# Ten tiles for weight parts, one plain block in the second passes, and side work two steps later in a one-core decoder layer

## The chip, the cores and the metric

The kernel runs on one core of a Trainium2 chip. The metric is the time of one execution on the device in microseconds (us); shown is the median of several executions. The engines are TensorE (PE), VectorE (DVE), ScalarE (ACT), GpSimd (POOL) and SyncE (SP). In this kernel SP issues nearly all transfers (DMAs), in one queue and in order; an issue that waits holds all that are behind it. The other engines, too, work through their instructions in the order of their queue.

## The reference, cut to what matters

One layer of a decoder is computed for 1024 prompt tokens and 64 sample tokens, in single precision:

```python
h = x + 0.5 * rms_norm(swiglu(rms_norm(x, g_f1_pre), w_f1_gu, w_f1_down), g_f1_post)
mix, k_new, v_new, s_new = mixer(rms_norm(h, g_m_pre), ...)
h = h + rms_norm(mix, g_m_post)
h = h + 0.5 * rms_norm(swiglu(rms_norm(h, g_f2_pre), w_f2_gu, w_f2_down), g_f2_post)

def swiglu(x, w_gu, w_down):
    g, u = jnp.split(x @ w_gu, 2, axis=-1)
    return (jax.nn.silu(g) * u) @ w_down
```

The model width is 1024, the hidden width of a SwiGLU 2816, that is 22 blocks of 128. The mixer (stick-breaking attention and retention) lies between the two SwiGLUs; the change touches nothing of it.

## The kernel before, in words

**Three matmuls for one.** Every operand is held as two parts, a high one in a rounded format and the rest. `hi` (L96, on ACT) makes the high part, `lo` (L99, mostly on DVE) the rest, and `mm3` (L133, L137, L138) does a product with three matmuls: high by high, high by low, low by high. To split a weight or an activation is thus one step on ACT and one on DVE.

**Passes and quarters.** A SwiGLU (`ffn`, L693) goes over the tokens in two passes, of 512 and 576 tokens. In a pass the input is cut into four quarters, B11, B21, B12 and B22: the upper or lower half of the model width by the first or second half of the tokens, 256 or 288 columns each. Two weight blocks (f and f + 1) make a round g; a pass has 11 rounds.

**Two kinds of block.** For a block f the product of the gate weights and of the up weights with the input is four quarters of weights by four of input. A *plain* block (`"S1" not in w`, in `swiglu_hidden`) splits four weight quarters, A11, A12, A21 and A22, and does 8 products of quarters. Any other block uses seven products: the weights give A11, A12, A22 and the sums S1 to S4, the input gives B11, B21, B22 and the sums T1 to T4. Each product of quarters is 4 x 3 = 12 matmuls. The weight sums are four operations (L589, L590, L591, L596) on POOL, for blocks 2 and 3 of a first pass on DVE. `PLAIN = 2` (L62) makes blocks 0 and 1 of either pass plain. Split weights go to tiles `sh` and `sl` (L572) in a ring of nine each. A block's generator gives way after its first half and after its second. A plain block has 4 products in either half; another has A11 B11, S2 T2, S3 T3 and S1 T1 in the first, A12 B21, A22 T4 and S4 B22 in the second.

**Where the T come from.** In a first pass DVE makes them from the quarters (`first_sums`, L260). For a second pass they are made on POOL during the first one (`sums`, L244; four operations L251, L253, L255 and L257 for each of four j), stored to the buffer `cB` in DRAM with the quarters, and loaded and split by `late` (L286). `late_sums` (L294) gives these loads in three steps: T2 and T3, T1, T4. T4 uses the buffer of quarter B12 (`HOME`), so it can be loaded only when no product reads B12 any more.

**Second products.** `down` (L706) multiplies a round's two hidden blocks by their rows of the down weights: for each of eight outputs d the products with the first and then with the second block, into banks `pc`; DVE adds the result to `y` (L719), or ACT copies it in the first round. `unit` (L140) loads 512 KB of these weights into a raw tile `wrd` (L146), one of two, and splits it into `whd` and `wld`. A round's `down` stands in the program one round later, between the halves of the next round's first block; only the first round's of a first pass comes before the weights of round 2.

**Side work.** Before the second half of each block a step of a generator is done on the side (`side1`, `side2`), from round 2 on: steps 0 to 19 in a pass. In the second SwiGLU's first pass these are two calls of `boundary` for the tokens of the second pass (norms: squares on ACT, L440, added up on DVE in `acc`, L442; then scaling on DVE, L538, and a sum on POOL or DVE, L540), 8 steps each, and `later_quarters` (L1752), 2 steps, which makes quarters and T for the second pass: 18 steps in all.

**What sets the order.** The program is written out in order, and a scheduler with its own model of durations sets each engine's queue from it; an instruction earlier in the program goes first when several are ready, so blocks and second products are interleaved. `beside` (L116) adds an order by hand: what a step makes on the named engines is put behind the last instruction that each of them had got until then. SP is not among the engines named. Tiles are given out in the scheduler's order, and a tile's next use waits for its last reader.

Of the kernel before, what the change touches and what calls it, by code (L numbers as in the profile page):

```python
# [12 lines left out]
F32R = mybir.dt.float32r  # L13
# [6 lines left out]
P = 128  # L20
# [38 lines left out]
B11, B21, B22, B12, T2, T3, T1, T4 = range(8)  # L59
QUARTERS = (B11, B21, B22, B12)  # L60
HOME = {T4: B12}
PLAIN = 2  # L62

# [3 lines left out]
class Trunk:  # L69
# [70 lines left out]
    def unit(self, src, pool=None, sfx="", eng=None, raw=None):  # L140

        nc = self.nc
        k, c = src.shape[1], src.shape[2]
        raw = self.t(self.wraw, [P, 1024], "wr", bufs=2) if raw is None else self.t(raw, [P, 1024], "wrd", bufs=2)
        rv = raw[:, : k * c].rearrange("p (k c) -> p k c", c=c)
        nc.sync.dma_start(rv, src)  # L146
        pool = pool or self.wsp
        h = self.t(pool, [P, 1024], "wh" + sfx, F32R)
        l = self.t(pool, [P, 1024], "wl" + sfx, F32R)
        self.hi(h[:, : k * c], raw[:, : k * c])  # L150
        self.lo(l[:, : k * c], raw[:, : k * c], h[:, : k * c], eng)
        return (h[:, : k * c].rearrange("p (k c) -> p k c", c=c),
                l[:, : k * c].rearrange("p (k c) -> p k c", c=c))
# [139 lines left out]

    def late_sums(self, u):  # L294
        yield {}
        for bs in ((T2, T3), (T1,), (T4,)):
            for b in bs:
                self.late(u, b)
            yield
# [258 lines left out]
            pass  # L558


    def swiglu_weights(self, wgu, f, adder):


        nc = self.nc
        g = self.t(self.wraw, [P, 1024], "wr", bufs=2)
        v = self.t(self.fw, [P, 1024], "wr2", bufs=2)
        nc.sync.dma_start(g.rearrange("p (k c) -> p k c", c=P), self.cols(wgu, f * P))
        nc.sync.dma_start(v.rearrange("p (k c) -> p k c", c=P), self.cols(wgu, FF + f * P))
        names = ("A11", "S2", "S3", "S1", "A12", "A22", "S4")
        if f < PLAIN:  # L570
            names = ("A11", "A12", "A21", "A22")
        out = {x: [self.t(self.sw, [P, 512], y, F32R, bufs=9) for y in ("sh", "sl")] for x in names}  # L572

        def split(name, src):
            h, l = out[name]
            self.hi(h, src)
            self.lo(l, src, h)
            out[name] = [x.rearrange("p (k c) -> p k c", c=P) for x in (h, l)]

        g0, g1, v0, v1 = g[:, :512], g[:, 512:], v[:, :512], v[:, 512:]  # L580
        tt = adder.tensor_tensor
        split("A11", g0)
        if f < PLAIN:
            split("A12", g1)
            split("A21", v0)
            split("A22", v1)
            return out
        split("A22", v1)
        tt(v1, v0, v1, op=ALU.add)  # L589
        tt(v0, g0, v0, op=ALU.subtract)  # L590
        tt(g0, v1, g0, op=ALU.subtract)  # L591
        split("S2", g0)
        split("S3", v0)
        split("S1", v1)
        split("A12", g1)
        tt(g1, g1, g0, op=ALU.subtract)  # L596
        split("S4", g1)
        return out
# [94 lines left out]
    def ffn(self, q, y, wgu, wdown, chunks, side, begin):  # L693

        nc = self.nc
        with self.fctx as ctx:
            with ExitStack() as ctx2:
                sums = begin(self.pool("fft", ctx2))  # L700
                next(sums)
            dp = self.pool("ffd", ctx, bufs=2)
            self.hp = self.pool("ffh", ctx, bufs=2)
            self.fs = self.pool("ffs", ctx)

            def down(p, g, dw, hid):  # L706
                o0 = PASSES[p][0]
                for o, n in chunks[p] if p or g + 2 < NF else ((0, 256), (256, 256)):
                    c = slice(o - o0, o - o0 + n)
                    for d in range(KD):  # L710
                        dd = slice(d * P, (d + 1) * P)
                        ps = self.bank("pc")
                        for j, ((wh, wl), (hh, hl)) in enumerate(zip(dw, hid)):
                            self.mm3(ps[:, :n], wh[:, 0, dd], wl[:, 0, dd], hh[:, c], hl[:, c],
                                     j == 0, j == len(dw) - 1)
                        if g == 0:
                            nc.scalar.activation(y[p][:, d, c], ps[:, :n], AF.Copy)
                        else:
                            nc.vector.tensor_tensor(y[p][:, d, c], y[p][:, d, c], ps[:, :n], op=ALU.add)  # L719

            for p, (o, n) in enumerate(PASSES):
                before = None
                for g in range(0, NF, 2):
                    if g == 2 and p == 0:
                        before()
                        before = None
                    gens = []
                    begun = {}
                    for f in (g, g + 1):
                        self.beside(lambda: gens.append(self.swiglu_hidden(self.swiglu_weights(  # L730
                            wgu, f, nc.vector if p == 0 and f in (PLAIN, PLAIN + 1) else nc.gpsimd), q, n)),
                            (mybir.EngineType.Activation,) if begun else (mybir.EngineType.DVE,) if self.scaled else (),
                            begun or self.scaled)
                        self.scaled = None
                        if f == 0:
                            next(gens[0])
                            begun = next(sums)
                    next(gens[1 if g == 0 else 0])
                    if before is not None:
                        self.pin = self.last_on(mybir.EngineType.PE)  # L740
                        before()
                        self.pin = None
                    hid = []
                    for i, gen in enumerate(gens):
                        if g == 0:
                            self.beside(lambda: next(sums))
                            if begun and i == 0:
                                begun = self.so_far()
                        else:
                            if i:  # L750
                                next(gen)
                            self.beside(lambda: side(p, g - 2 + i))
                        hid.append(next(gen))
                    if g == 0:
                        self.beside(lambda: next(sums))
                    dw = []
                    for f in (g, g + 1):
                        self.beside(lambda: dw.append(self.unit(
                            wdown[f * P : (f + 1) * P, :].rearrange("p (k c) -> p k c", k=1), pool=dp, sfx="d",
                            raw=self.fw)), PINNED if begun else (), begun)  # L760
                    before = partial(down, p, g, dw, hid)
                if p == 0:
                    q = {}, {}
                    for b in QUARTERS:
                        self.late(q, b)
                    sums = self.late_sums(q)
                before()
# [782 lines left out]
    def mixer_out(self):  # L1550
        nc, io = self.nc, self.io
        mch = [(0, 512), (512, 288), (800, 288)]
        with ExitStack() as ctx:
# [50 lines left out]
            for d in OUT_FIRST:  # L1604
                ws[d] = unit(d)
                product(0, ws[d], d)
# [9 lines left out]
    def run(self):  # L1616
        nc, io = self.nc, self.io
# [22 lines left out]
        todo = {}  # L1640
# [19 lines left out]
        with ExitStack() as mctx:  # L1660
# [16 lines left out]
            y, pl, yc = self.mixer_out()  # L1677


        q = self.left()  # L1680

        def second_boundary(p, o, n, tags):
            c = slice(o - PASSES[p][0], o - PASSES[p][0] + n)
            return self.boundary(pl, y[p][:, :, c], o, n, self.h1T, gain["g_mix_post"], gain["g_ffn2_pre"], self.h2T,
                                 lambda *x: None, tags)
# [52 lines left out]
        def side2(p, i):  # L1738
            if p == 0:
                if i == 0:  # L1740
                    todo["ends"] = chain.from_iterable(
                        [second_boundary(1, o, 288, ("pm", "pm")) for o in (512, 800)]
                        + [later_quarters()])
                next(todo["ends"], None)
            else:
                if i == 0:
                    todo["ends"] = chain.from_iterable([stages(0, o, 256, "pc") for o in (0, 256)])
                if next(todo["ends"], todo) is todo and todo["rows"] < len(tail):
                    residual_rows(todo["rows"])
                    todo["rows"] += 1  # L1750
# [123 lines left out]
```

## Time and profile before

| | |
|---|---|
| median of 3 runs | 2871.73 us (2867.34 to 2874.34) |
| the profiled execution | 2862.49 us, span 2860.0 us |
| PE busy | 2779.8 us, 97% of the span, 20064 matmuls |
| DVE busy | 2012.3 us, 70% |
| ACT busy | 1244.4 us, 44% |
| POOL busy | 737.5 us, 26% |
| DMA | 380.63 MB, mean 133 GB/s |
| mean granted PE clock | 0.990 |

The first SwiGLU fills the span's beginning: its first pass runs to about 375 us, its second to about 780. The second SwiGLU runs from about 2067 us to the end, its second pass from about 2425. Matmuls overlap: each takes 280 to 290 ns by its row, while the next starts 120 to 130 ns after it, so distances between starts are read, not durations. A bracket behind a row is the idle time of the engine before it, with what ended that.

### The profile page before, as it was taken

The page shows a single profiled execution, that of the slowest core. Times are in us where ns is not written, and L with a number is a line of the kernel's source. Part 1 is how long each engine was busy: PE and PEld are TensorE (multiplying, and loading weights), DVE is VectorE, ACT ScalarE, POOL GpSimd, SP SyncE. Part 2 cuts the span into 40 slices and gives each one's busy share as a digit, 9 for nine tenths or more (in the row PEclk, how much of TensorE's full clock was granted, in tenths as well). Part 3 has the DMA queues.
Part 4 walks back from the last instruction along what each step waited for, and adds up shares of the span by engine and source line. Part 5 has one row for each costly group of instructions (what it writes and reads, how often), then busy time and mean ns, then how long its engine had stood idle before and what let it go on. Part 6 is the DMA issues. An engine that isn't in the chain of part 4 may idle for free.

```text
span 2860.0 us, 51596 instructions
## 1 busy us (share of the span) xinstructions
PE 2779.8 (97%) x20064; PEld 2638.2 (92%) x20064; DVE 2012.3 (70%) x3918; ACT 1244.4 (44%) x2550; POOL 737.5 (26%) x677
## 2 busy tenths in 40 slices
PE   8999999999999999999999999999999999999998
PEld 7898899999989999989999888878989988999997
DVE  7888878888753644544889844445488898688776
ACT  6544444434343333334666642323354444544433
POOL 0234513333150000000001136530113434233331
PEclk9999999999999999999999999999999999999999
DMA  6434444333252323333223379986234346333421
GB/s 186 146 122 146 141 155 125 105 113 111 69 159 88 109 74 92 100 95 102 74 67 88 116 246 334 335 302 190 89 102 132 118 124 197 108 106 102 129 88 38
DMA packets 420868, 380.63 MB, mean 133 GB/s; under 512 B 30800, under 2 KB 381392, under 8 KB 420624
## 3 DMA queue, kind: packets, MB, share of 16 engines
q1 hardware_dynamic: 398352, 306.03, 34.8%
q0 software_dynamic: 22272, 71.31, 7.4%
q8 instruction: 157, 2.57, 0.4%
q14 instruction: 87, 0.71, 0.1%
HBM read 310.03 MB, written 63.05 MB: 130 GB/s over the span
## 4 chain that ended last, share of the span: by engine, by line
PE 61%; DVE 4%; DMA 2%; issue 1%; POOL 1%; ACT 0%; SPq 0%; DVEq 0%; ACTq 0%; POOLq 0%
PE pa L133 10%; PE pa L138 10%; PE pa L137 10%; PE pb L133 4%; PE pb L138 4%; PE pb L137 4%; PE pc L137 3%; PE pc L138 3%; PE pc L133 3%; PE pc L1224 2%; PE pm L1013 1%; PE pm L1129 1%; PE pb L1129 1%; PE pc L1001 1%; DVE sl L99 1%
## 5 line engine op out<-in xcount | busy, mean ns | idle before, releaser
L96 ACT ACTIVATE sh<-wr 128x512 fp32r<-128x512 f32 x592 | 339.3, 622 | 358.4 <-POOL wr L591 136.9
L133 PE MATMUL pa<-uh,wh 128*128 128x384 f32 (+1 forms) x1408 | 471.1, 335 | 4.2 <-ACT qdec L922 2.1
L138 PE MATMUL pa<-uh,wl 128*128 128x384 f32 (+1 forms) x1408 | 465.6, 331 | 0.0
L137 PE MATMUL pa<-ul,wh 128*128 128x384 f32 (+1 forms) x1408 | 464.0, 330 | 0.4 <-POOL ul L99 0.4
L99 DVE TENSOR_TENSOR sl<-wr,sh 128x512 fp32r<-128x512 f32 x592 | 398.2, 699 | 58.5 <-ACT sh L96 55.0
L133 PE MATMUL pa<-q,sh 128*128 128x256 f32 (+1 forms) x1408 | 409.2, 291 | 15.5 <-DVE p L649 7.7
L137 PE MATMUL pa<-q,sh 128*128 128x256 f32 (+1 forms) x1408 | 408.6, 290 | 2.2 <-DVE q L99 2.2
L138 PE MATMUL pa<-q,sl 128*128 128x256 f32 (+1 forms) x1408 | 407.3, 289 | 0.3 <-DVE sl L99 0.3
L137 PE MATMUL pc<-hl,whd 128*128 128x256 f32 (+2 forms) x1088 | 350.4, 324 | 2.6 <-DVE hl L99 2.6
L138 PE MATMUL pc<-hh,wld 128*128 128x256 f32 (+2 forms) x1088 | 349.9, 323 | 0.0
L133 PE MATMUL pc<-hh,whd 128*128 128x256 f32 (+2 forms) x1088 | 343.6, 324 | 4.5 <-DVE y L719 2.5
L719 DVE TENSOR_TENSOR y<-y,pc 128x256 f32<-128x256 f32 (+2 forms) x496 | 249.7, 515 | 134.5 <-PE pc L138 133.0
L133 PE MATMUL pb<-q,sh 128*128 128x288 f32 (+1 forms) x1088 | 314.7, 290 | 6.4 <-ACT sh L96 4.8
L138 PE MATMUL pb<-q,sl 128*128 128x288 f32 (+1 forms) x1088 | 314.4, 289 | 0.5 <-DVE sl L99 0.4
L137 PE MATMUL pb<-q,sh 128*128 128x288 f32 (+1 forms) x1088 | 314.7, 289 | 0.0
L133 PEld LDWEIGHTS pa<-q,sh 128*128 128x128 f32 x1408 | 266.9, 190 | 20.7 <-DVE p L649 8.7
L133 PEld LDWEIGHTS pa<-uh,wh 128*128 128x128 f32 x1408 | 266.5, 189 | 12.3 <-ACT qdec L922 3.2
L137 PEld LDWEIGHTS pa<-q,sh 128*128 128x128 f32 x1408 | 266.7, 189 | 4.9 <-DVE q L99 2.9
L137 PEld LDWEIGHTS pa<-ul,wh 128*128 128x128 f32 x1408 | 266.1, 189 | 2.0 <-POOL ul L99 0.7
L138 PEld LDWEIGHTS pa<-uh,wl 128*128 128x128 f32 x1408 | 265.8, 189 | 2.1 <-issue 1.2
L138 PEld LDWEIGHTS pa<-q,sl 128*128 128x128 f32 x1408 | 265.9, 189 | 1.5 <-DVE sl L99 0.6
L589 POOL TENSOR_TENSOR wr<-wr 128x512 f32<-128x512 f32 x76 | 108.5, 1428 | 497.4 <-DVE sl L99 493.5
(372 smaller groups left out, 5944.6 us busy)
## 6 DMA issues: line engine op xcount, KB each, us to landing
wr<-in_w_ffn_gu_dram SPq DMA_DIRECT2D x176, 512.0 KB
wrd<-in_w_ffn_down_dram SPq DMA_DIRECT2D x88, 512.0 KB
wr<-in_w_in_dram SPq DMA_DIRECT2D x56, 512.0 KB
q<-cB SPq DMA_DIRECT2D x16, 576.0 KB
wr<-in_w_o_dram SPq DMA_DIRECT2D x10, 512.0 KB
cB<-y SPq DMA_DIRECT2D x32, 144.0 KB
cB<-xr SPq DMA_DIRECT2D x32, 144.0 KB
s<-in_state_ret_dram SPq DMA_DIRECT2D x16, 256.0 KB
```

What stands on the lines that cost most here:

```text
L96: return self.nc.scalar.activation(dst, src, AF.Copy)
L99: (eng or self.nc.vector).tensor_tensor(dst, src, hi.bitcast(F32), op=ALU.subtract)
L133: ins = mm(ps, wh, xh, start=first, stop=False)
L137: mm(ps, wh, xl, start=False, stop=False)
L138: mm(ps, wl, xh, start=False, stop=last)
L589: tt(v1, v0, v1, op=ALU.add)
L719: nc.vector.tensor_tensor(y[p][:, d, c], y[p][:, d, c], ps[:, :n], op=ALU.add)
L1001: nc.tensor.transpose(tp[:, j * P : (j + 1) * P], bt[:, j * P : (j + 1) * P], self.ident)
L1013: ins = nc.tensor.matmul(po[:, lo:256], vs[:, j, :], ats[j // 4][x][:, j % 4, lo:256], start=(j == 0 and x == 0), stop=(j == last and x == 1))
L1129: return nc.tensor.matmul(out[32 * m : 32 * m + 32], w(m), x(m), start=first, stop=last, skip_group_check=True)
L1224: ins = nc.tensor.transpose(tp[:, i * P : (i + 1) * P], kp[i // 2][:, (i % 2) * 512 + m * P : (i % 2) * 512 + (m + 1) * P], self.ident)
```

## The change

Four things are changed.

- The rings of `sh` and `sl` get ten tiles and no longer nine; the raw tiles `wrd` of the second products are one and no longer two (the pool's own number).
- In second passes only block 0 is plain. Block 1 is of the other kind, with its weight sums on POOL, so T2, T3 and T1 are asked for together in the first of the three steps, T4 in the second, and the third is empty. In a second pass block 1's first half now stands after block 0's second half and not before it.
- In `swiglu_weights` the number of plain blocks is handed over; blocks 2 and 3 of first passes make their sums on DVE as before.
- In the second SwiGLU's first pass the side work does nothing in steps 0 and 1, so it stands one round later.

```diff
-PLAIN = 2
+PLAIN = 2, 1
...
-        raw = ... if raw is None else self.t(raw, [P, 1024], "wrd", bufs=2)
+        raw = ... if raw is None else self.t(raw, [P, 1024], "wrd")
...
-        for bs in ((T2, T3), (T1,), (T4,)):
+        for bs in ((T2, T3, T1), (T4,), ()):
...
-        if f < PLAIN:
+        if f < plain:
             names = ("A11", "A12", "A21", "A22")
-        out = {x: [self.t(self.sw, [P, 512], y, F32R, bufs=9) for y in ("sh", "sl")] for x in names}
+        out = {x: [self.t(self.sw, [P, 512], y, F32R, bufs=10) for y in ("sh", "sl")] for x in names}
...
-                            wgu, f, nc.vector if p == 0 and f in (PLAIN, PLAIN + 1) else nc.gpsimd), q, n)),
+                            wgu, f, nc.vector if p == 0 and f in (2, 3) else nc.gpsimd, PLAIN[p]), q, n)),
...
-                    next(gens[1 if g == 0 else 0])
+                    if g or p == 0:
+                        next(gens[1 if g == 0 else 0])
...
                     for i, gen in enumerate(gens):
                         if g == 0:
+                            if p and i:
+                                next(gen)
                             self.beside(lambda: next(sums))
...
-                next(todo["ends"], None)
+                if i > 1:
+                    next(todo["ends"], None)
```

## Rows read from the trace of the kernel before

**Rows 1.** The page: busy time of each engine; the chain that ended last, by engine.
```profile
PE 2779.8 (97%) x20064; PEld 2638.2 (92%) x20064; DVE 2012.3 (70%) x3918; ACT 1244.4 (44%) x2550; POOL 737.5 (26%) x677
...
PE 61%; DVE 4%; DMA 2%; issue 1%; POOL 1%; ACT 0%; SPq 0%; DVEq 0%; ACTq 0%; POOLq 0%
```

**Rows 2.** Busy time by stretch: length, PE, PEld, DVE, ACT, POOL, clock, DMA.
```profile
60.00:410.00 350.00, 342.10 (x2406) 320.68 (x2405) 288.13 (x479) 155.47 (x304) 122.95 (x93) 1.00 0.46 145
2090.00:2130.00 40.00, 34.62 (x228) 31.76 (x228) 36.84 (x77) 26.83 (x58) 4.01 (x3) 0.96 0.37 118
2130.00:2430.00 300.00, 292.26 (x2026) 270.71 (x2025) 262.19 (x459) 130.03 (x260) 122.43 (x97) 1.00 0.45 139
2440.00:2820.00 380.00, 380.00 (x2881) 379.97 (x2880) 289.81 (x548) 163.51 (x316) 117.10 (x90) 1.00 0.31 94
...
2126.00:2130.00 4.00, 4.00 (x24) 4.00 (x24) 2.42 (x7) 1.56 (x4) 0.00 (x0) 0.61 0.00 0
```

**Rows 3.** Timeline from 2118.9: start, us, engine, line, operation.
```profile
2118.91 1.40 DVE L663 TENSOR_TENSOR hf<-hf,c 128x256 f32<-128x256 f32 x1
...
2120.11 1.36 POOL L590 TENSOR_TENSOR wr<-wr,wr 128x512 f32<-128x512 f32 x1
...
2120.24 1.55 DVE L442 TENSOR_TENSOR acc<-acc,sq 128x288 f32<-128x288 f32 x1
...
2123.11 0.45 DVE L442 TENSOR_TENSOR acc<-acc,sq 128x288 f32<-128x288 f32 x1
...
2123.81 0.45 DVE L442 TENSOR_TENSOR acc<-acc,sq 128x288 f32<-128x288 f32 x1
...
2124.52 0.41 DVE L649 TENSOR_TENSOR p<-pa,u 128x256 f32<-128x256 f32 x1
...
2124.99 0.38 PE L133 MATMUL pa<-q,sh 128*128 128x256 f32 x1 [3.61 <-DVE p L649]
```

**Rows 4.** Timeline of PE in a second pass, twelve matmuls apart.
```profile
2457.61 0.30 PE L133 MATMUL pa<-q,sh 128*128 128x288 f32 x1
...
2459.21 0.30 PE L133 MATMUL pa<-q,sh 128*128 128x288 f32 x1
```

**Rows 5.** Timeline of SP, ACT and DVE: T4 of the second SwiGLU's second pass.
```profile
2462.47 0.33 SPq L290 DMA_DIRECT2D q<-cB  x1
...
2467.45 1.17 ACT L96 ACTIVATE q<-q 128x1152 fp32r<-128x1152 f32 x1
...
2470.63 2.45 DVE L99 TENSOR_TENSOR q<-q,q 128x1152 fp32r<-128x1152 f32 x1
```

**Rows 6.** The chain from 2286 to 2300: start, us, what.
```profile
2291.74 3.94 DMA wr<-in_w_ffn_gu_dram
```

**Rows 7.** Groups by line: count, busy us, mean ns, idle before.
```profile
L96 ACT ACTIVATE whd<-wrd 128x1024 fp32r<-128x1024 f32 x88 | 92.2, 1052 | 69.1 <-PE pc L137 68.6
```

**Rows 8.** Timeline of DVE and PE: second products' weights, at 2096 and 2316.
```profile
2096.08 1.22 DVE L99 TENSOR_TENSOR wld<-wrd,whd 128x1024 fp32r<-128x1024 f32 x1
...
2097.69 0.40 PE L133 MATMUL pc<-hh,whd 128*128 128x512 f32 x1
...
2316.68 2.31 DVE L99 TENSOR_TENSOR wld<-wrd,whd 128x1024 fp32r<-128x1024 f32 x1
...
2334.13 0.39 PE L133 MATMUL pc<-hh,whd 128*128 128x512 f32 x1
```

**Rows 9.** Timeline of POOL: first and last of 16 sums, and block 21's last.
```profile
2374.87 1.00 POOL L251 TENSOR_TENSOR xr<-y 128x288 f32<-128x288 f32 x1
...
2396.27 1.01 POOL L257 TENSOR_TENSOR xr<-y,xr 128x288 f32<-128x288 f32 x1
...
2410.47 1.29 POOL L596 TENSOR_TENSOR wr<-wr 128x512 f32<-128x512 f32 x1 [5.13 <-DVE sl L99]
```

**Rows 10.** Waits of PE from 2380 to 2405: us in total, times, longest.
```profile
PE pb L133 <- ACT sh L96: 1.4, 1, 1.4
```

**Rows 11.** The chain, near the change of passes in the second SwiGLU.
```profile
2422.52 8.39 DMA q<-cB
```

More of the change, by code (lines that the diff above doesn't have):

```diff
@@ L143, in unit @@
         k, c = src.shape[1], src.shape[2]
-        raw = self.t(self.wraw, [P, 1024], "wr", bufs=2) if raw is None else self.t(raw, [P, 1024], "wrd", bufs=2)
+        raw = self.t(self.wraw, [P, 1024], "wr", bufs=2) if raw is None else self.t(raw, [P, 1024], "wrd")
         rv = raw[:, : k * c].rearrange("p (k c) -> p k c", c=c)
@@ L558, in all, with swiglu_weights @@
             pass
-    def swiglu_weights(self, wgu, f, adder):
+    def swiglu_weights(self, wgu, f, adder, plain):
         nc = self.nc
@@ L582, in swiglu_weights @@
         split("A11", g0)
-        if f < PLAIN:
+        if f < plain:
             split("A12", g1)
```

## The prediction

> **What bounds the kernel now.** First the share of busy time and the chain that ended last: TensorE (PE) is busy 97% of the span, and PE alone is 61% of the chain; the next engine is at 4% [rows 1]. So only fewer matmuls, or fewer moments in which PE stands still, shorten the kernel. Then the stretches of the two SwiGLUs [rows 2]: span minus PE's busy time is 350.0 - 342.1 = 7.9 us in most of the first SwiGLU's first pass, 40.0 - 34.6 = 5.4 us at the second one's beginning, 300.0 - 292.3 = 7.7 us in the rest of its first pass, and nothing at all in its second pass, where PE is busy 380.00 of 380.00. Second passes are matmul time; first passes lose some 20 us to waits, and there VectorE (DVE) is the busiest of the feeders: 36.8 of 40 us at the beginning, 262 of 300 after it.
>
> The largest wait is 3.61 us at 2124.99, for DVE [rows 3]. The reader is to see there what DVE did: it ran one queue in which side work stood between the block's own steps, `acc` (L442), and two of them, L663 and `acc`, took 1.40 and 1.55 us, beside a sum of GpSimd (POOL), L590, where other `acc` took 0.45. After the wait the granted clock was 0.61 in the mean over 2126 to 2130 [rows 2], so for most of it at the lower of its two levels, 1.2 and not 2.4 GHz.
>
> **The sum is made against the profiled execution**, 2862.49 us, of which 2860.0 are its span. The median of the three timed runs is 2871.73, or 9.2 us above it; I carry the difference over to the median.
>
> **One plain block in the second passes.** A plain block is 8 products of 12 matmuls, the other form 7. Each second pass loses 12 matmuls of 288 columns. Twelve of them start in 2459.21 - 2457.61 = 1.60 us [rows 4], and PE has no gap there to hide it in: 2 x 1.60 = -3.2 us. For it, weight block 1 now needs three splits more on ScalarE (ACT) and DVE, and four sums on POOL, and its halves some more steps on DVE. DVE has 90 us free in 380 [rows 2], POOL 263, so nothing.
>
> **T4 comes closer.** T4 shares a buffer with quarter B12, which the plain block reads until its third product of the second half; the load then waits for that. Before, T4 was needed only in block 2's second half. Now it is needed in block 1's: after 12 + 48 + 12 matmuls, 72 x 0.133 = 9.6 us. What has to happen: 5.0 us from issue to ACT's split, 1.17 us for that, and the DVE split, which began 3.2 us after ACT's began and took 2.45 us, together 10.6 us [rows 5]; undisturbed, DVE's split needs less. It is also queued behind block 1's last step on DVE (L653). Behind the issue on SP stand the next weight loads. Nothing waits there now, so it can't gain; between 0 and 3 us per SwiGLU; I take 0.5, as the two lengths are almost equal: +1.0.
>
> **One raw buffer for the second products' weights.** Now the second load goes out when DVE has split the first, and not one round ahead. No row shows such a pair; the nearest: a 512 KB load held a chain for 3.94 us [rows 6], ACT's split is 1.05 us by its mean [rows 7], DVE's 1.22 us in one place and 2.31 in another [rows 8]. So the second part is ready 3.9 + 1.1 + 1.2 to 2.3 = 6.2 to 7.3 us after the first, plus DVE's queue. In the middle of a first pass the first split ends at 2316.68 + 2.31 = 2318.99 and the products begin at 2334.13 [rows 8]: 15 us, hidden. At the beginning there is no such lead: the first split ends at 2097.30 and the product with the second part stands at 2097.69. PE will find some other matmuls (block 2's first products, the first part's share), not 7 us of them, as the sums T that these read are still being made on DVE. Between 0 and 6 us at either beginning; I take 1.5 each, +3.0, nearer to nothing because a delay there also moves block 3 away from the burst of rows 3. On SP the waiting load holds what is behind it, the next gate weights, which have their own two buffers.
>
> **Side work two steps later.** The second SwiGLU's first pass makes 18 side steps, which now fill steps 2 to 19 instead of 0 to 17; none is dropped. At the beginning, three `acc` operations leave DVE's queue ahead of L649: 1.55 + 0.45 + 0.45 = 2.45 us [rows 3], so the 3.61 us wait shrinks to some 1.2, and of the slow clock (4 us at 0.61, or some 1.5 us) I count 1.0 back: -3.4 (bounds 0 and -5.4, the whole loss of the stretch in rows 2). At the end, the 16 POOL sums that ran from 2374.87 to 2397.28 [rows 9] move one round later, behind block 21's last weight sum, which was at 2410.47. Beside them, PE once waited 1.4 us for a split whose sum stood behind them in POOL's queue [rows 10]; in the new place block 0 of the second pass needs no such sums: -1.0 (bounds -1.4 and 0). But they end near 2410 + 22 = 2432, where the second pass begins. Their 16 stores stand in SP's queue with the loads of the quarters. One of these took 8.39 us in the chain, beside three loads of T parts [rows 11]; those now come later, which frees it, while the queue may hold it. Between -1.5 and +5; I take +0.5.
>
> **The tenth tile.** A part of the next block can be written one product earlier. Where PE waits for ACT `sh` in the first passes this helps, in the second it is worth nothing. Between +1 and -5 (a third of the 15.6 us in rows 2); I take -1.0, as the waits shown are for DVE's queue, which a tile does not shorten.
>
> **Sum:** -3.2 + 1.0 + 3.0 - 3.4 - 1.0 + 0.5 - 1.0 = -4.1 us; 2858.4 for a run like the profiled one, **2867.6 us** for the median. That is 0.14%. A measurement here can tell some 0.3% (8.6 us) from no change, so the likeliest outcome is a small gain that can't be told.
>
> The row of DVE beside POOL is borne out by the Trainium skill, SBUF - State Buffer, section "Who interferes with whom": a VectorE instruction with two SBUF inputs contends with a GpSimd instruction that reads SBUF. By that rule the 22 us of POOL sums are not free wherever they are put, and this change puts them beside the second pass's first splits; the trace agrees in rows 3. What it would give is rival C.
>
> **Rivals.**
> A. *The first passes lose their waits.* With side work away from the beginning and a tile more, half of the 15.6 us and all but 1 us of the 5.4 us go: -3.2 + 1 - 7.8 - 4.4 = -14.4, so 2857.3. For it: three separate loosenings at the engine that is late. Against: the first SwiGLU's side work is not moved, and DVE has as much to do as before.
> B. *The single raw buffer decides, and it is slower.* If the second load is not issued at once, because SP stands at another wait, or ACT reaches the second split before the load lands, then ACT stands, and behind it the next `sh` and `hh` splits on which PE waits. Price: it decides where the first split ends less than some 10 us before the products begin (3.94 + 1.05 + 2.31 and about 3 of DVE's queue). Half of the ten rounds of a first pass losing 1.5 us, in two SwiGLUs, is 15 us, with 6 us at the beginnings; less 3.2 for matmuls and 3.4 for the beginning: +14, so 2886. Against: the 15 us of rows 8.
> C. *The sums collide at the change of passes.* L663 and L442 took about 1 us more beside POOL; five such on PE's path, and the +5 us of SP's queue, take what the move gives: -4.1 + 5.0 + 4.5 = +5.4, so 2877.
> D. *The work is moved and nothing is late.* Only the matmuls count: -3.2, 2868.5; no different in size from the forecast.
>
> **How the numbers follow.** Forecast and D together 0.42, A 0.34, B 0.14, C 0.10. Faster by over 0.3% (below 2863.1): A nearly whole and some of the forecast's lower side, 0.38. Slower by over 0.3% (above 2880.3): B and a part of C, 0.19. Between: 0.43. The low end takes A's value and the bounds beyond it: 2850; the high end C's value and the near side of B: 2882. The forecast's own range is 2861 to 2874.
>
> **What would show it.** 24 matmuls fewer. PE still busy throughout the second passes from some 25 us after their start; a gap before the product with T4 of 0 to 1 us. No `acc` before the second round of the second SwiGLU; the wait for L649 near 2125 under 1.5 us and the clock at 1.00 behind it. At both beginnings a new wait of `pc` matmuls for `whd` or `wld`, under 3 us, and none later in the pass. The POOL sums after block 21's L596, with PE's wait for quarters under 2 us. I am wrong if ACT waits on the load of `wrd` in most rounds (B), if the gap at the change of passes is over 4 us (C), or if the first passes together show under 10 us of PE gaps (A).

## The result, and the profile after

The changed kernel took 2876.87 us in the median of 17 runs (2871.29 to 2882.31); the kernel before, run beside it, 2869.39 (2863.30 to 2874.69, 17 runs). The ratio is 1.0027 with a 95% interval of 1.0019 to 1.0035: the change makes the kernel slower by 0.27%, about 7.7 us. Forecast were 4.1 us less. The profiled execution took 2881.15 us, span 2879.4.

One profiled execution differs from the next by several us even where nothing was changed: the mixer, from the last product of the first SwiGLU to the first of the second, took 1280 to 1289 us over the traces here. So verdicts come from medians; the traces say where to look.

The page after: busy time by engine, and the chain by engine.

```profile
PE 2789.2 (97%) x20040; PEld 2641.5 (92%) x20040; DVE 2047.6 (71%) x3934; ACT 1248.2 (43%) x2558; POOL 758.8 (26%) x685
...
PE 56%; DVE 7%; DMA 2%; issue 2%; POOL 1%; ACT 1%; SPq 0%; DVEq 0%; ACTq 0%; POOLq 0%
```

There are 24 matmuls fewer than in [rows 1], as the diff says. DVE's busy time grew by 35.3 us for 16 instructions more: its instructions grew longer. In the chain PE lost five points and DVE won three.

Busy time by stretch, columns as in [rows 2], with 410 to 770 us added, and the sum over the five; first the kernel after, then the kernel before for the added stretch and the sum.

```profile
60.00:410.00 350.00, 340.58 (x2387) 316.91 (x2386) 303.20 (x488) 163.15 (x314) 132.00 (x97) 1.00 0.47 146
410.00:770.00 360.00, 355.64 (x2659) 354.45 (x2659) 293.74 (x559) 149.92 (x302) 114.62 (x89) 1.00 0.34 102
2090.00:2130.00 40.00, 39.60 (x282) 36.64 (x281) 33.57 (x72) 24.93 (x53) 2.72 (x2) 1.00 0.41 126
2130.00:2430.00 300.00, 289.43 (x1998) 266.56 (x1997) 267.35 (x463) 131.99 (x270) 112.28 (x90) 1.00 0.39 120
2440.00:2820.00 380.00, 375.29 (x2818) 373.69 (x2818) 300.45 (x548) 167.62 (x323) 131.45 (x96) 0.99 0.37 112
sum 1430.00, PE 1400.53 PEld 1348.26 DVE 1198.32 ACT 637.61 POOL 493.08; mean PE 280.11 PEld 269.65 DVE 239.66 ACT 127.52 POOL 98.62
```

```profile
410.00:770.00 360.00, 359.72 (x2706) 358.81 (x2705) 294.43 (x567) 154.37 (x310) 115.09 (x89) 1.00 0.33 102
...
sum 1430.00, PE 1408.71 PEld 1361.94 DVE 1171.39 ACT 630.21 POOL 481.57; mean PE 281.74 PEld 272.39 DVE 234.28 ACT 126.04 POOL 96.31
```

PE lost 8.2 of its 1408.7 busy us in the same stretches. That is near the 7.7 us of the medians, though these two traces lie 19.4 us apart, 5 of them in the mixer. The beginning won 5.0 us (34.62 to 39.60); all the others lost, both second passes above all (4.1 and 4.7), where PE had stood still for almost nothing before. Of the 4.7, 3.6 us are two waits at the change of passes (at 2445.24 and 2446.88): this pass begins at 2434.5 here and at 2423.5 before, so the change of passes lies inside the stretch only here. By the sum in this last row the traces of the kernels below are compared: it falls where PE waits.

A new wait is seen at ACT's split `whd`: what ended the idle time before it, us and times. Before, that was a product of PE alone [rows 7].

```profile
  DMA wrd<-in_w_ffn_down_dram: 63.4, 39
  PE pc L137: 37.6, 24
```

The longest new wait of PE in the SwiGLUs' rounds, from 60 us on, is at 493.92. The timelines of DVE, POOL and PE there, start and duration in us:

```profile
489.75 2.31 DVE L99 TENSOR_TENSOR wld<-wrd,whd 128x1024 fp32r<-128x1024 f32 x1
491.98 1.51 DVE L663 TENSOR_TENSOR hf<-hf,c 128x288 f32<-128x288 f32 x1
493.42 0.45 DVE L667 TENSOR_TENSOR hf<-pb,u 128x288 f32<-128x288 f32 x1
...
489.62 1.35 POOL L590 TENSOR_TENSOR wr<-wr,wr 128x512 f32<-128x512 f32 x1
491.05 2.13 POOL L591 TENSOR_TENSOR wr<-wr,wr 128x512 f32<-128x512 f32 x1
...
493.92 0.49 PE L133 MATMUL pb<-q,sh 128*128 128x288 f32 x1 [2.56 <-DVE hf L667]
```

The next product's bank `pb` is free when L667 has read it. L667 takes 0.45 us, but it stands behind the second weights' split `wld` and behind L663. Beside the sums L590 and L591 these took 2.31 and 1.51 us, where `wld` takes 1.225 by its median and L663 0.459. Without the lengthening L667 would have begun 1.09 + 1.05 = 2.1 us earlier by this estimate, and of the 2.56 us some 0.4 were left. The wait costs more than itself, as the one in [rows 3] did. The 4 us behind it, columns as in [rows 2]:

```profile
494.00:498.00 4.00, 4.00 (x20) 4.00 (x21) 2.74 (x7) 3.16 (x7) 0.00 (x0) 0.57 0.29 111
```

The granted clock is 0.57 in the mean there, so for most of the stretch at 1.2 and not 2.4 GHz, and 20 matmuls begin where 30 would at the distance of [rows 4]. PE counts as busy meanwhile, so the sum above leaves this out.

### The profile page after: what moved, and what is told of

It is laid out like the page before. It is cut to its first block, busy times and chain, and to the rows that moved or that the text cites. A ratio compares the mean times of both kernels' runs of the same rounds, so it can differ in the third digit from the quotient of the medians.

```text
span 2879.4 us, 51504 instructions
## 1 busy us (share of the span) xinstructions
PE 2789.2 (97%) x20040; PEld 2641.5 (92%) x20040; DVE 2047.6 (71%) x3934; ACT 1248.2 (43%) x2558; POOL 758.8 (26%) x685
## 4 chain that ended last, share of the span: by engine, by line
PE 56%; DVE 7%; DMA 2%; issue 2%; POOL 1%; ACT 1%; SPq 0%; DVEq 0%; ACTq 0%; POOLq 0%
PE pa L133 10%; PE pa L138 9%; PE pa L137 9%; PE pb L133 3%; PE pb L137 3%; PE pb L138 3%; PE pc L137 2%; PE pc L138 2%; PE pc L133 2%; PE pc L1227 2%; DVE sl L99 1%; PE pm L1016 1%; DMA wrd<-in_w_ffn_down_dram 1%; PE pm L1132 1%; PE pb L1132 1%
## 5 line engine op out<-in xcount | busy, mean ns | idle before, releaser
L99 DVE TENSOR_TENSOR sl<-wr,sh 128x512 fp32r<-128x512 f32 x598 | 404.3, 700 | 77.4 <-ACT sh L96 74.6
L133 PE MATMUL pb<-q,sh 128*128 128x256 f32 (+1 forms) x1080 | 312.7, 290 | 4.1 <-DVE hf L667 2.6
L137 PE MATMUL pb<-q,sh 128*128 128x256 f32 (+1 forms) x1080 | 313.6, 290 | 0.1
L138 PE MATMUL pb<-q,sl 128*128 128x256 f32 (+1 forms) x1080 | 311.8, 289 | 0.0
```

Source lines behind the costliest of these rows:

```text
L99: (eng or self.nc.vector).tensor_tensor(dst, src, hi.bitcast(F32), op=ALU.subtract)
L133: ins = mm(ps, wh, xh, start=first, stop=False)
L137: mm(ps, wh, xl, start=False, stop=False)
L138: mm(ps, wl, xh, start=False, stop=last)
```

## The experiments

All were timed against the kernel before; given is the ratio with its 95% interval. "One raw tile" means the single `wrd`.

**One part at a time.**

Two raw tiles and rings of nine in the kernel after (one plain block and the shift remain):

```diff
-        raw = ... "wrd")
+        raw = ... "wrd", bufs=2)
...
-        out = ... bufs=10) ...
+        out = ... bufs=9) ...
```

> The changed kernel with two raw tiles for the second products and rings of nine again; one plain block and the later side work are kept. Theory R (the single raw buffer costs): the waits of ScalarE for the load of wrd (63.4 us in 39 waits in the changed kernel) go to nothing, and the kernel is faster than before by 3 to 8 us (3.2 of matmuls, the rest at the second SwiGLU's beginning), so 10 to 15 us below the changed one. Theory P (the new beginning of the second passes costs, by T4, the quarters and the sums): the loss stays, 4 to 8 us slower than before. Theory Q (no part costs by itself, each edit only reorders the queues): within 3 us of before.

Measured: 1.0006 (0.9995 to 1.0017). Without the two changes of tiles the loss is gone, and no gain is left.

One raw tile in the kernel before, the first line of that diff the other way round:

> The kernel before with one raw tile for the second products' weights and no other edit. Theory R: slower than before by 9 to 16 us, with the waits of ScalarE for the load of wrd as in the changed kernel, some 40 of them. Theory P: within 2 us of before, the waits there but hidden. Theory Q: within 3 us.

Measured: 1.0007 (0.9997 to 1.0017). ACT waits for the load of `wrd` as in the kernel after, and on balance it costs next to nothing:

```profile
ACT whd L96 <- DMA wrd<-in_w_ffn_down_dram: 68.3, 38, 7.7
...
ACT whd L96 <- PE pc L137: 54.2, 23, 10.6
```

The shift alone, in the kernel before:

```diff
-                next(todo["ends"], None)
+                if i > 1:
+                    next(todo["ends"], None)
```

> The kernel before with the second SwiGLU's side work two steps later and no other edit. Theories R and Q: faster by 2 to 5 us, the wait near 2125 us gone, the second pass's beginning not later by more than 1 us. Theory P: the sums at the change of passes cost 3 to 5 us there, so within 2 us of before or slower.

Measured: 0.9994 (0.9982 to 1.0005).

One plain block in second passes alone (the first diff, and the two lines of the shift taken back):

> The kernel before with one plain block in the second passes (and the T parts and block 1's first half placed as this asks for), with nine tiles, two raw tiles and the side work where it was. Theory R: faster by 2 to 4 us, its matmuls. Theory P: slower by 3 to 6 us, with gaps of 2 to 3 us before T4's product and at the first quarters in either second pass. Theory Q: within 3 us.

Measured: 1.0002 (0.9992 to 1.0012). So three parts cost nothing that can be told, each by itself. The tenth tile was left.

**The tenth tile.**

The kernel after with rings of nine, all else kept:

> The changed kernel with rings of nine tiles again; single raw buffer, one plain block and later side work are kept. So far the changed kernel is 7.5 us slower than before, without the single buffer and the tenth tile it is 0 to 5 us slower by its interval, and the single buffer alone adds -1 to +5. Theory X (the single buffer costs more beside the other two edits, the tenth tile nothing): 6 to 9 us slower than before. Theory Y (the tenth tile costs, as ScalarE takes splits of a later block first): at most 4 us slower than before.

Measured: 0.9999 (0.9987 to 1.0011). Two of its stretches, columns as above:

```profile
410.00:770.00 360.00, 356.26 (x2666) 353.86 (x2665) 293.79 (x560) 150.24 (x305) 117.85 (x92) 1.00 0.34 101
2130.00:2430.00 300.00, 293.72 (x2047) 272.58 (x2046) 269.73 (x471) 134.17 (x271) 125.75 (x99) 1.00 0.43 130
```

From 410 to 770 us, where the wait at 493.92 stands, the tenth tile makes next to no difference (355.64 with it); from 2130 to 2430 it takes 4.3 us (289.43). So in the changed kernel the jam shown above is not where the tenth tile costs. In the stretch where it does, PE waits 3.1 us in three places for ACT's copy `p` (L643), for which it waits once without the tile, 0.4 us. One of the three, in the kernel after, by the timelines of ACT and PE:

```profile
2303.07 1.06 ACT L96 ACTIVATE whd<-wrd 128x1024 fp32r<-128x1024 f32 x1 [2.87 <-DMA wrd<-in_w_ffn_down_dram]
...
2304.36 1.66 ACT L96 ACTIVATE sh<-wr 128x512 fp32r<-128x512 f32 x3
...
2306.57 0.36 ACT L643 ACTIVATE p<-pa 128x256 f32<-128x256 f32 x1
...
2306.98 0.39 PE L133 MATMUL pa<-q,sh 128*128 128x256 f32 x1 [0.99 <-ACT p L643]
```

The copy stands in ACT's queue behind a split that waited 2.87 us for the load of `wrd`, and behind three weight splits. That a tenth tile lets such splits go first is argued from these rows.

The kernel before with one raw tile and rings of ten:

> The kernel before with one raw buffer and rings of ten, nothing else. Theory X: as with the single buffer alone, 1 to 3 us slower than before. Theory Y: 4 to 8 us slower, with gaps of PE in the first SwiGLU's passes as in the changed kernel.

Measured: 1.0037 (1.0024 to 1.0051). Taking the tenth tile away takes the loss away; adding it to the single raw tile brings all of it. PE's busy time in the five stretches, with one raw tile and nine tiles, then ten:

```profile
sum 1430.00, PE 1406.81 PEld 1355.14 DVE 1168.81 ACT 630.89 POOL 489.28; mean PE 281.36 PEld 271.03 DVE 233.76 ACT 126.18 POOL 97.86
```

```profile
sum 1430.00, PE 1401.34 PEld 1352.61 DVE 1189.75 ACT 632.10 POOL 490.03; mean PE 280.27 PEld 270.52 DVE 237.95 ACT 126.42 POOL 98.01
```

DVE is busy 20.9 us more with the same work, PE 5.5 us less. In the second's trace the jam of 489.75 us above is found again, at 2544.33, with one raw tile and the tenth tile as its only changes. DVE, POOL and PE:

```profile
2544.33 2.31 DVE L99 TENSOR_TENSOR wld<-wrd,whd 128x1024 fp32r<-128x1024 f32 x1
2546.57 1.51 DVE L663 TENSOR_TENSOR hf<-hf,c 128x288 f32<-128x288 f32 x1
2548.00 0.45 DVE L667 TENSOR_TENSOR hf<-pb,u 128x288 f32<-128x288 f32 x1
...
2544.20 1.36 POOL L590 TENSOR_TENSOR wr<-wr,wr 128x512 f32<-128x512 f32 x1
2545.64 2.12 POOL L591 TENSOR_TENSOR wr<-wr,wr 128x512 f32<-128x512 f32 x1
...
2548.50 0.40 PE L133 MATMUL pb<-q,sh 128*128 128x288 f32 x1 [2.73 <-DVE hf L667]
```

It is there a second time at 2656.78, with a wait of 2.73 us. With a third wait for L667, of 3.64 us at 2401.89 behind other steps, PE waits 9.1 us for L667 in this kernel; with nine tiles no such wait is over 0.72 us. Long steps alone are no loss: `wld` takes over 1.8 us 7 times in the kernel before, 18 times with one raw tile, which costs next to nothing, and 27 times with the tenth tile too (22 in the changed kernel).

**Side work elsewhere**, two attempts at a better version. The kernel before with steps 0 and 1 empty and made up for by two steps each at 4 and 8:

```diff
-                next(todo["ends"], None)
+                if i > 1:
+                    next(todo["ends"], None)
+                if i in (4, 8):
+                    next(todo["ends"], None)
```

> The kernel before with side steps 0 and 1 left empty in the second SwiGLU's first pass and two steps made at 4 and at 8, so that the sums T are made where they were. If the later side work gains at the beginning and loses at the change of passes (shift alone: first pass 4.9 us shorter, second 1.4 longer in its profile): 3 to 6 us faster than before, with PE's wait for the first quarters under 1.2 us. If the beginning's gain is lost again in the rounds that make two steps: within 2 us of before.

Measured: 0.9994 (0.9985 to 1.0003). And with only steps 16 and 17 moved, behind the last weight sums (`if i not in (16, 17)`):

> The kernel before with only the two steps that make quarters and T moved, from 16 and 17 to 18 and 19. If these collide with the change of passes: 1 to 3 us slower than before, with waits of PE for the quarters' splits of 2 to 3 us. If they don't: within 1 us of before, since the beginning is untouched.

Measured: 0.9992 (0.9981 to 1.0003). Neither can be told from no change.

**Does the tenth tile need the single raw tile?** Ten tiles and two raw ones don't fit, so space was made at `xr`, the tiles of the side sums, and measured by itself:

```diff
-"xr", bufs=6
+"xr", bufs=4
```

> The kernel before with four and not six small tiles xr for the side work, which frees 2.5 KB a partition; nothing else. It is the base for the next run. Both theories: within 4 us of before.

> The same with rings of ten tiles, and two raw buffers. Single buffer and tenth tile together cost 0.37% (10 us), the single buffer alone 0.07%. Theory Y1 (the tenth tile alone costs): 5 to 10 us slower than the kernel with four xr, VectorE 20 to 30 us busier. Theory Y2 (it costs only beside the single buffer, as two queues get late together): within 3 us of the kernel with four xr.

Measured: 1.0016 (1.0006 to 1.0027) with nine tiles and 0.9995 (0.9986 to 1.0004) with ten. Beside two raw tiles the tenth does no harm. Against its own base it rather helps, but that base is itself 0.16% slower than the kernel before by an edit meant to be neutral. Yet DVE's steps grew longer there too:

```profile
PE 2785.2 (97%) x20064; PEld 2644.4 (92%) x20064; DVE 2034.5 (71%) x3918; ACT 1244.4 (43%) x2550; POOL 741.0 (26%) x677
```

With the same instructions it was 2012.3 us in [rows 1] and 2014.1 in the base. So a longer busy DVE alone is not yet a loss of time; it is one if PE waits behind the step that grew.

**Does it need sums that read?** One raw tile, and POOL's four weight sums replaced by operations that only write (the weight sums are left out):

```diff
+        def tt(out, a, b, op):
+            if adder is nc.gpsimd:
+                adder.memset(out, 0.5)
+            else:
+                adder.tensor_tensor(out, a, b, op=op)
```

> The kernel before with the single raw buffer, and GpSimd's four weight sums of a block replaced by a memset of the same tile, which reads nothing; the weight sums of those blocks are left out of the computation. Order and waits of the steps are kept. Theory K (collisions of GpSimd's sums with VectorE's two-input steps are what PE waits for): VectorE some 80 us less busy, the first passes' gaps down by half, 8 to 15 us faster than before. Theory L (ScalarE's waits for the load cost, collisions are hidden): within 4 us of before.

> The same with rings of ten. Theory K: the tenth tile's cost goes with the collisions, so within 2 us of the run with nine. Theory L: the 8 us that the tenth tile costs stay.

Measured: 0.9912 (0.9897 to 0.9927) with nine, 0.9918 (0.9905 to 0.9931) with ten. The tenth tile's 0.30% beside one raw tile shrinks to 0.06%, inside the intervals. With ten tiles, DVE's busy time with sums that read and with writes alone:

```profile
PE 2786.8 (97%) x20064; PEld 2643.9 (92%) x20064; DVE 2038.6 (71%) x3918; ACT 1248.4 (43%) x2550; POOL 750.0 (26%) x677
```

```profile
PE 2774.2 (98%) x20064; PEld 2636.2 (93%) x20064; DVE 1919.9 (68%) x3918; ACT 1248.4 (44%) x2550; POOL 477.3 (17%) x677
```

The same 3918 instructions are 118.7 us shorter; with nine tiles it is 94.7 us (2009.6 to 1914.9). Writes take POOL less time too, so this run alone doesn't part "reads nothing" from "is shorter".

**Is it the late second split, and which ring?** The kernel after with `wrd` in two halves, each loaded and split by itself:

```diff
...
+            for o in (0, 512):
+                half = self.t(raw, [P, 512], "wrd", bufs=2)
+                nc.sync.dma_start(half, src[:, 0, o : o + 512])
+                self.hi(h[:, o : o + 512], half)
+                self.lo(l[:, o : o + 512], half, h[:, o : o + 512], eng)
...
```

> Kernel after with the down weights' raw tile as two tiles of half the size (512 columns, 256 KB): each half is loaded and split by itself, so the second block's first half loads while the first block's second half is still being split; ten tiles and the space stay, 44 splits more on ACT and as many on DVE. Theory Y2 (the tenth tile costs only beside a single buffer, because the second wld split then comes late and between the block's own steps): ratio to before 0.998 to 1.000, so 0.3 to 0.5% under the kernel after; ACT's waits for the load of wrd fall from some 63 us to under 15. Theory K alone (the tenth tile lengthens DVE's steps beside GpSimd whatever the raw tiles do): 1.002 to 1.004, like after.

Measured: 0.9985 (0.9974 to 0.9997), 0.42% below the kernel after. The time came out as expected of the late split, the reason given for it did not. ACT's wait for the load is as large as before (66.8 us, 61 times; 63.4 and 39 in the kernel after). What did change is the length of a piece of DVE work:

```profile
L99 DVE TENSOR_TENSOR wld<-wrd,whd x176: 672/687/1789, 52.6 to 2822.4; 128x512 fp32r<-128x512 f32 x176
```

```profile
L99 DVE TENSOR_TENSOR wld<-wrd,whd x88: 1206/1225/2326, 52.6 to 2841.9; 128x1024 fp32r<-128x1024 f32 x88
```

These are `wld` with halves and in the kernel after, minimum, median and maximum in ns: a critical step stands behind a piece of 1.8 us at most, and not of 2.3.

Ten tiles for `sh` and nine for `sl`, beside one raw tile in the kernel before:

```diff
-... bufs=9) for y in ("sh", "sl")] ...
+... bufs=b) for y, b in (("sh", 10), ("sl", 9))] ...
```

> Kernel before with the single raw tile, ten tiles for the high parts sh and nine for the low parts sl. If the tenth tile costs because ACT runs a product ahead and meets the wait for the raw load earlier in its queue: 1.003 to 1.005, as with ten of both. If it costs because DVE's low splits come earlier and between the block's own steps: 1.000 to 1.001, as the ring of sl is still nine.

Measured: 1.0020 (1.0011 to 1.0028), between the two answers, with an interval that overlaps those of nine tiles (1.0007) and of ten (1.0037). ACT's ring alone seems to carry a part of the cost. No wait of PE for L667 is over 0.70 us here, so this part does not go by the jam on DVE.

**All weight sums on DVE**, in the kernel after and in the kernel before:

```diff
-... nc.vector if p == 0 and f in (2, 3) else nc.gpsimd ...
+... nc.vector ...
```

> Kernel after with all weight sums on DVE, none on GpSimd (0.69 us each by the row of blocks 2 and 3, in place of 1.35 us on GpSimd). DVE gets some 78 x 4 x 0.69 = 215 us more, and loses the some 110 us by which its steps are longer beside GpSimd: busy 2150, 75%. Theory K (it is DVE's steps beside GpSimd's sums that PE waits for): 0.991 to 0.997, and no worse than the kernel before with the same edit. Rival (DVE's queue is what is late, so more work in it costs): 1.005 to 1.02.

> Kernel before with all weight sums on DVE. Theory K: 0.991 to 0.997. Rival (DVE's queue): 1.004 to 1.02. The difference to the kernel after with the same edit is what the change costs without any sum on GpSimd: theory K and Y2 together 0.0 +- 0.1%; if the change's cost is the late load alone, +0.2 to +0.3%.

Measured: 0.9968 (0.9955 to 0.9980) after, 0.9961 (0.9947 to 0.9975) before. The change costs 0.07% there, inside the intervals; both are faster than the kernel before. DVE's busy time in the latter is 2082.3 us: 70 more, for 304 sums that take 0.68 us each or 207 in all; by this estimate some 137 us had been lengthening. Its stretches, columns as above:

```profile
60.00:410.00 350.00, 347.43 (x2471) 327.32 (x2470) 308.46 (x566) 161.28 (x314) 24.66 (x18) 1.00 0.48 150
410.00:770.00 360.00, 355.65 (x2674) 354.28 (x2674) 308.30 (x641) 151.70 (x303) 10.28 (x12) 1.00 0.34 101
```

The first pass won 5.3 us of PE's time, the second lost 4.1. Hence the last two: sums on DVE in first passes only (`nc.vector if p == 0 else nc.gpsimd`), in the kernel before and in the one with halves.

> Kernel before with the weight sums of first passes on DVE, those of second passes on GpSimd as before. With all sums on DVE the first passes were 9 to 11 us shorter each in the profile, the second passes 3 to 5 us longer. If these are separate effects: 0.992 to 0.995, faster than with all sums on DVE (0.9961). If the second passes lost their time only because the shorter first passes hand over less prepared work, no better than 0.996.

> Kernel after with the down weights' raw tile in two halves and the weight sums of first passes on DVE. If the change, once its late load is mended, gives a small gain of its own (half_raw measured 0.9985), it adds to the gain of the sums: 0.990 to 0.994, below the kernel before with the same sums. If the gain of half_raw was the same waits that the sums take away: 0.994 to 0.997, no better than the other.

Measured: 0.9950 (0.9936 to 0.9964) and 0.9968 (0.9956 to 0.9979). The first has the lowest time here of the kernels that do the whole computation, faster than both kernels; its interval overlaps that of all sums on DVE in the kernel before:

```profile
60.00:410.00 350.00, 347.37 (x2451) 326.50 (x2449) 307.09 (x563) 161.00 (x315) 30.82 (x22) 1.00 0.48 149
410.00:770.00 360.00, 358.92 (x2698) 357.74 (x2698) 297.28 (x571) 152.78 (x308) 114.99 (x88) 1.00 0.34 101
...
sum 1430.00, PE 1417.70 PEld 1371.80 DVE 1211.09 ACT 638.48 POOL 291.10; mean PE 283.54 PEld 274.36 DVE 242.22 ACT 127.70 POOL 58.22
```

The first pass keeps its gain, the second is back near the kernel before (359.72). The second version, with the change and its loss mended, is no better: the gain of the halves did not add up, and the change is worth nothing on top of the sums.

## Why the prediction was wrong, by its steps

**The step that failed is the tenth tile, -1.0 us with bounds of +1 and -5.** Beside one raw tile it measured +0.30% (1.0007 to 1.0037) and +0.28% (0.9999 to 1.0027), some 8 us; beside two raw tiles -0.21% (1.0016 to 0.9995), some -6. I priced the tile and the raw buffer as two terms of a sum. They are one: what the first costs hangs on the second. (That it gains beside two raw tiles is less sure, as that base is 0.16% above the kernel before, and ten tiles beside it measured 0.9995.) My reason, that a tile does not shorten the waits for DVE's queue, was nearly the point; I did not ask whether it makes a queue worse. The traces show two ways in which it can: `wld` and the next block's sums on POOL meet in front of L663 and L667, and ACT's copy `p` stands behind a split that waits for the load and behind further splits. Without the tenth tile the forecast is -3.1 us or -0.11%, and the kernel after with nine tiles measured -0.01% (-0.13 to 0.11): the rest of the sum is neither contradicted nor shown.

What is shown: the loss needs the tenth tile (it is gone with nine), and one raw tile (with two it is gone), in one piece (with halves it is gone), and the sums on POOL (with writes only, and with the sums on DVE, it is within the error). The three kernels that hold all four (one of them with ten tiles in one ring only) lost 0.20 to 0.37%. What is not shown: by which chain of queue positions the tenth tile costs, and how much of the loss goes by either way above. PE's waits for L667 are 9.1 us with the two changes of tiles alone, but 2.6 us in the changed kernel, and there in a pass that the tenth tile did not lengthen. The scheduler orders every queue anew with each edit, and an edit meant to be neutral moved the time by 0.16% (`xr` with four tiles). That the halves help through shorter pieces on DVE is argued from one pair of rows.

**One raw buffer, +3.0.** Alone it measured 0.07% (-0.03 to 0.17), some 2 us: right in size, but by luck. I had the loss at the beginnings, and there the second SwiGLU won 3.7 us in its trace (34.62 to 38.35); what was lost, 4.8 us, was lost from 410 to 770 us (359.72 to 354.90), where I had none. ACT's waits for the load came not at the beginnings only, but in most rounds (39 waits in the changed kernel). Rival B named that sign ("ACT waits on the load of `wrd` in most rounds") and it came; its price, +14, did not: ACT has the time, busy 43%. So the sign that I set for B told nothing about the time.

**Matmuls and T4, -3.2 and +1.0.** One plain block alone measured +0.02% (-0.08 to 0.12); -2.2 us is -0.08%, at the interval's end, so it can't be told apart. T4 came without a wait of PE: in the second SwiGLU's second pass its split on DVE ended at 2477.36, and from 2465 to 2490 no idle time is listed before a matmul.

```profile
2466.55 1.17 ACT L96 ACTIVATE q<-q 128x1152 fp32r<-128x1152 f32 x1 [3.85 <-PE pb L138]
...
2476.01 1.35 DVE L99 TENSOR_TENSOR q<-q,q 128x1152 fp32r<-128x1152 f32 x1
```

The -3.2 rested on second passes without gaps [rows 2], and the change put gaps there; the single raw tile alone did so too.

**The shift, -3.4 at the beginning.** The wait of 3.61 us [rows 3] is gone and the clock stands at 1.00 from 2126 to 2130. But with the single raw tile alone, without the shift, PE is busy 38.35 of these 40 us too: the wait was one that other edits also dissolve. Alone the shift measured -0.06% (-0.18 to 0.05), where my three terms give -3.9 us, -0.14%: inside the interval, so neither shown nor refuted. In its trace the beginning won 2.3 us (36.92 of 40).

**The change of passes, +0.5 and -1.0.** Here I was too low. The first 35 us of the second SwiGLU's second pass, after and then before, and PE's wait for a quarter in the former:

```profile
2434.50:2469.50 35.00, 30.51 (x211) 29.32 (x210) 26.75 (x40) 16.41 (x25) 17.85 (x14) 0.90 0.70 239
```

```profile
2424.00:2459.00 35.00, 33.77 (x264) 33.33 (x263) 20.50 (x39) 11.20 (x18) 3.88 (x3) 1.00 0.45 151
```

```profile
2445.24 0.40 PE L133 MATMUL pa<-q,sh 128*128 128x288 f32 x1 [2.46 <-ACT q L96]
```

PE lost 3.3 us there, and the clock fell to 0.90 in the mean; 53 matmuls fewer begin, or some 7 us at the distance of [rows 4], an estimate. That is rival C's place, and most of its price of 9.5 us. Yet C is not what decided: the kernel with two raw tiles and rings of nine, which has the shift, loses there too (31.43 us busy, clock 0.95) and nothing that can be told on the whole. In its trace the second SwiGLU's first pass is 4.7 us shorter than before and the second 4.9 us longer: the gain and the cost were both larger than forecast, and that they cancel was not foreseen.

The Trainium skill, SBUF - State Buffer, section "Who interferes with whom", says that a VectorE instruction with two SBUF inputs contends with a GpSimd instruction that reads SBUF. The traces agree: `wld` took 2.31 us beside L590 and 1.225 in the median, L667 with one input in PSUM never more than 0.46. I used the rule for one place, the change of passes; long steps beside POOL's sums stand in the rounds too.

## What to carry to other kernels

Ask of a buffer that lets work run ahead what it will run into: two edits that share a queue (here ACT's and DVE's) have one price together, not two. Where one engine's steps stand beside another's reads, read minimum, median and maximum of an instruction, and look for what waits behind the longest. A listed wait of an engine that has time to spare, such as ACT's 68 us for the load, is no loss by itself; it becomes one where a step that PE needs stands behind it, as at 2306.98. And look where two versions differ, pass by pass, before the longest wait is taken for the cause.

## What the runs showed of the hardware

Sums on POOL lengthen DVE's two-input steps up to some three times (L663: 0.450 us in the median, 1.474 at most in the kernel before), 95 to 137 us of DVE's time in all by the three pairs above; with writes in their place, which also take POOL less time, 0.9% of the kernel's time comes back. DVE does such a sum in 0.68 us and POOL in 1.3 to 1.35. Giving DVE those of the first passes made the kernel faster (0.9950); giving it those of the second passes too brought nothing more (0.9961).
